# Two pieces of elementwise work in a decoder's mixers, moved from VectorE to GpSimd

## The chip, the core and the metric

The kernel runs on one core of a Trainium2 chip. The metric is the device time of one execution in microseconds (us). The engines named below are TensorE (PE: matmuls), VectorE (DVE), ScalarE (ACT), GpSimd (POOL) and SyncE (SP), which here only issues DMAs. Each engine runs its own list of instructions strictly in order; between engines there are semaphore waits.

## What is computed

One step of a two-layer decoder trunk for 256 prompt tokens and 64 sample tokens (8 sequences of 8). A layer is a SwiGLU feed-forward block, a block of four parallel mixers, and a second feed-forward block. The mixers read one input projection and feed one output projection:

```
proj = modulate(x, sh2, sc2) @ w_in[l]
u, v, xb, gate_b, gate_c, hc, glu_a, glu_g = split(proj)
ya = gelu(u) * (tril(w_s) @ layer_norm(gelu(v), ln_g, ln_b) + b_s)   # A
yb = (window_mean(xb, 2|4|8|16) - xb) @ pool_w * pool_scale          # B
yc = gate_b * conv3(gate_c * hc)                                     # C
yd = silu(layer_norm(conv31(glu_a * sigmoid(glu_g)) + b))            # D
x  = layer_norm(alpha*x + (1+g2) * rms_norm([ya|yb|yc|yd]) @ w_out[l])
```

The change touches two pieces: the running sums behind B's window means (each of four channel groups has its own window, 2, 4, 8 or 16 tokens), and the scale and offset `ln_g`, `ln_b` of A's values `v`.

## The kernel before

Activations lie with channels on the 128 partitions and the 320 tokens along the free axis. All weights are streamed from HBM once. Each weight unit (128 x 1024, fp32) is cut by ACT (L232, `whi`) and DVE (L240, `wlo` = `raw` - `whi`) into a high and a low part, and each product of TensorE is three matmuls. The weight units of the input projection are cut several units ahead of the matmuls that use them, and the order of all instructions is the order in which the Python code issues them; no scheduler moves them.

In a mixer block the projection's first five column groups are done together (`zcm`): D's two halves and the first half of B's input. ScalarE and VectorE form D's gated input `eD`, `cD` (L906 to L910), and ScalarE lays out a halo copy of it and makes tap 0 of the 31-tap convolution: `dtap0` (L914, L915), first for channel half 0, then for half 1, into the two accumulators `aD`. The other 30 taps of each half are 60 DVE instructions (L923), alternating between the halves, each reading `cD` and `aD` and adding into `aD`. ScalarE also copies B's input to `eB`, `eBs` (L940, L941).

The rest of the input projection is ten weight units: `hc0`, `xb1`, `up0`, `val` (two), `up1`, `gc0`, `gb0`, `gc1`, `hc1`, `gb1`. The list `MIX_SEQ` writes their order out by hand, with the other steps between them. At each new weight unit a hook adds to a `credit` the time that TensorE will need for the unit, less the cost of a split, and issues taps until the credit is used up; each step of `MIX_SEQ` then takes its price in `DVE_COST` off the credit. So the prices decide between which other DVE instructions the taps stand. The step `mean` issues all taps that are left, and then TensorE's matmuls `cmn` (L1116), which need both finished accumulators; TensorE issues nothing else until they are through. Behind `mean` come D's normalisation, C's taps, the group norms and the output projection `wo`.

The steps that the change touches:

- `pool0` and `pool1` (L946 to L969): for one channel half, the running sums over 2, 4 (or 2, 4, 8, 16) tokens by doubling, for prompt (L958) and samples (L959), and from them B's means less the input (L962 to L969). All on DVE. `pool0` stands first in `MIX_SEQ`, `pool1` far behind `mean`.
- `vgain` (`v_gain`, L1019): three tiles of 128 x 256 times `sgln[0]`, then plus `sgln[1]`: six DVE instructions, behind `mean`.
- `vstat`, `vnorm`: the values' statistics on DVE, a `pow` on POOL (L1012), then one DVE instruction (L1015) and three ScalarE instructions (L1017).

POOL does before the change only `pow` of 128 x 3 elements (L1012, L1132, L596, L367), four `affine_select` in the whole program (L438, L440), and memsets.

Of the kernel before, what the change touches and what calls it, by code (L numbers as in the profile page):

```python
# [67 lines left out]


MIX_SEQ = """  # L70
    pool0 hc0 xb1 up0 val vstat up1 gc0 gb0 vnorm cconv0 gc1 hc1 gb1 mean cconv1 sub sq4 ada6 ctaps0 ctaps1 cgate0
    cgate1 stat4 pow4 vgain ada2 sq2 bc4 norm swish stat2 sq3 sgu pow2 pool1 ada2 stat3 bc2 pow3 poolmm mul2 hi2
    sq1 sgate bc3 lo2 sq0 ada2 stat1 mul3 hi3 pow1 ko0 stat0 lo3 pow0 bc1 mul1 ko1 hi1 lo1 step step bc0 mul0 hi0
    ada18 ko2 lo0 ko3 ko4 ko5
""".split()
# [216 lines left out]
def sam(ap):  # L292
    return ap.rearrange("p (b t) -> p b t", t=NT_S)


class Kern:
# [568 lines left out]
    def mix_body(self, l, gb, G, late):  # L865
        nc, st, io, tp, mp = self.nc, self.st, self.io, self.t, self.mp
# [77 lines left out]

        yA, yB, yC, pl, gu, mix, vs = [], [], [], [], [], {}, {}

        def pool(j):
            e, es = eB[j], eBs[j]
            o = Y(f"pl{l}{j}")
            pl.append(o)  # L950
            sp = [mp.tile([P, 271], F32, tag="sp", bufs=2, name=f"s{i}p{l}{j}") for i in range(2)]
            ss = [mp.tile([P, NB, 23], F32, tag="ss", bufs=2, name=f"s{i}s{l}{j}") for i in range(2)]
            cp, cs_, sh = e, es, 1
            for g in range(2 * j + 2):
                np_, nss = sp[g % 2], ss[g % 2]
                lo = sh * 2 - 1
                p0 = 0 if g < 2 * j + 1 else 64
                V.tensor_tensor(np_[p0:P, lo:271], cp[p0:P, lo:271], cp[p0:P, lo - sh:271 - sh], op=ALU.add)  # L958
                V.tensor_tensor(nss[p0:P, :, lo:23], cs_[p0:P, :, lo:23], cs_[p0:P, :, lo - sh:23 - sh], op=ALU.add)  # L959
                if g // 2 == j:  # L960
                    q = slice(64 * (g % 2), 64 * (g % 2) + 64)
                    V.tensor_tensor(o[q, 0:16], np_[q, 15:31], self.inv[q, j, 0:16], op=ALU.mult)  # L962
                    V.scalar_tensor_tensor(o[q, 16:NP_], np_[q, 31:271], self.inv[q, j, 16:17], e[q, 31:271],
                                           op0=ALU.mult, op1=ALU.subtract)
                    V.scalar_tensor_tensor(sam(o[q, NP_:N]), nss[q, :, 15:23], self.inv[q, j, 16:17],
                                           es[q, :, 15:23], op0=ALU.mult, op1=ALU.subtract)
                cp, cs_ = np_, nss
                sh *= 2
# [12 lines left out]
        vb = []
# [37 lines left out]
        def v_gain():  # L1019
            for i, op in ((0, ALU.mult), (1, ALU.add)):  # L1020
                for b in range(3):
                    V.tensor_tensor(vb[b], vb[b], self.sgln[:, i, :], op=op)
            outs.append((io["o_vp"][l], vb[1]))
            outs.append((io["o_vs"][l], vb[2][64:128, :]))

# [144 lines left out]
        def taps_(n):  # L1170
            for _ in range(min(n, len(taps))):
# [4 lines left out]
               "gc": win(cgin), "hc": win(chin), "gb": win(cbin), "vstat": lambda _: v_stat(),  # L1176
               "vnorm": lambda _: v_norm(), "cconv": cconv, "t": taps_, "mean": mean, "sub": sub, "sq": sq, "stat": stat, "pow": pw_, "bc": bc, "mul": mul, "hi": hi, "lo": lo,
               "norm": norm, "swish": swish, "ctaps": ctaps, "cgate": cgate, "vgain": lambda _: v_gain(),
               "pool": pool, "poolmm": lambda _: pool_mm(), "sgu": lambda _: spatial(),
               "sgate": lambda _: spatial_gate(), "ko": ko, "ada": ada, "step": lambda _: self.ada_step()}  # L1180
        for nme, arg in MIX_OPS:
            ops[nme](arg)
            self.credit -= DVE_COST.get(nme, 0.0)
        st.ada(999)
# [245 lines left out]
```

## Time and profile before

| What | Value |
|---|---|
| device time, 3 runs | 1285.9 us median (1285.89 to 1292.28) |
| the profiled execution | 1289.18 us |
| its span, first to last instruction | 1287.4 us |
| mean granted TensorE clock | 0.99 |
| PE busy / DVE busy | 98% / 57% of the span |
| ACT busy / POOL busy | 43% / 2% of the span |
| layer 0: D's gated input done, `mean` on TensorE | 302.93 us, 350.96 us |
| layer 1: the same | 926.11 us, 975.46 us |

The span is 1.8 us shorter than the device time of the same execution, and that execution is 3.3 us above the median. Times within the trace count from the span's start. A row of the timeline gives the start, the duration, the engine, the line, the operation and the tiles; "x9" is nine equal instructions in a row, with the duration from the first's start to the last's end; the square bracket tells how long the engine was idle before, and whose instruction ended that.

### The profile page before, as it was taken

What the parts mean: (1) busy time and instruction counts of PE and PEld (TensorE: products, weight loads), DVE (VectorE), ACT (ScalarE), POOL (GpSimd) and SP (SyncE); (2) the same over time, 40 slices, a digit from 0 to 9 for tenths busy, and PEclk for the clock granted to TensorE, in tenths of its full rate; (3) what the DMA queues carried; (4) which work ended last, traced back from release to release, by engine and by line L of the source; (5) the groups of instructions that cost most, each with busy time, mean ns of one, the idle gap of its engine ahead of it and who ended that gap; (6) DMA issues with size and microseconds to landing.
All of it is one profiled execution on the core that took longest, in us unless ns stands there. A gap on an engine that the chain in (4) does not pass through costs nothing.

```text
span 1287.4 us, 22297 instructions
## 1 busy us (share of the span) xinstructions
PE 1263.3 (98%) x9414; PEld 1213.7 (94%) x9414; DVE 730.0 (57%) x1321; ACT 555.8 (43%) x872; POOL 22.4 (2%) x39
## 2 busy tenths in 40 slices
PE   9999999999999999999999999999997999999996
PEld 8999999999888999999999999999995989999996
DVE  5644444468977644453575454445798775454444
ACT  3643333347444643343445343333653455343332
POOL 0000000000010000000000000000000000000000
PEclk9999999999999999999999999999998989999999
DMA  9865556568849854534465555454775694434301
GB/s 376 315 233 211 196 198 255 198 213 240 303 182 94 327 180 148 211 135 162 164 216 209 173 187 201 176 201 171 222 256 197 104 236 164 155 140 164 131 1 41
DMA packets 63748, 247.46 MB, mean 192 GB/s; under 512 B 31072, under 2 KB 33632, under 8 KB 34464
## 3 DMA queue, kind: packets, MB, share of 16 engines
q1 hardware_dynamic: 58912, 245.11, 56.9%
q8 instruction: 74, 1.21, 0.4%
q10 hardware_dynamic: 4736, 0.93, 0.4%
q14 instruction: 26, 0.21, 0.0%
HBM read 243.45 MB, written 2.57 MB: 191 GB/s over the span
## 4 chain that ended last, share of the span: by engine, by line
PE 90%; DVE 6%; ACT 2%; DMA 1%; issue 1%; POOL 0%; ACTq 0%; another core or an unknown queue 0%; SPq 0%; DVEq 0%
PE of L672 4%; PE adp L466 4%; PE oh L673 4%; PE of L673 4%; PE oh L674 4%; PE of L674 4%; PE oh L672 4%; PE uf L672 4%; PE uh L674 4%; PE uh L672 4%; PE uf L673 4%; PE uf L674 4%; PE uh L673 4%; PE gf L672 4%; PE gh L672 3%; PE gh L674 3%
## 5 line engine op out<-in xcount | busy, mean ns | idle before, releaser
L240 DVE TENSOR_TENSOR wlo<-raw,whi 128x1024 fp32r<-128x1024 f32 x312 | 373.1, 1223 | 137.3 <-ACT whi L232 136.4
L232 ACT CAST whi<-raw 128x1024 fp32r<-128x1024 f32 x312 | 315.3, 1045 | 24.4 <-issue 8.4
L672 PE MATMUL of<-hhf,whi 128*128 128x320 f32 x352 | 109.4, 311 | 0.0
L674 PE MATMUL of<-hhf,wlo 128*128 128x320 f32 x352 | 108.9, 310 | 0.0
L673 PE MATMUL of<-hlf,whi 128*128 128x320 f32 x352 | 108.9, 309 | 0.0
L672 PE MATMUL oh<-hhh,whi 128*128 128x320 f32 x352 | 108.5, 308 | 0.0
L674 PE MATMUL oh<-hhh,wlo 128*128 128x320 f32 x352 | 108.5, 308 | 0.0
L673 PE MATMUL oh<-hlh,whi 128*128 128x320 f32 x352 | 108.5, 308 | 0.0
L672 PE MATMUL uf<-xhif,whi 128*128 128x320 f32 x320 | 99.3, 310 | 0.0
L672 PE MATMUL uh<-xhih,whi 128*128 128x320 f32 x320 | 98.9, 309 | 0.0
L674 PE MATMUL uf<-xhif,wlo 128*128 128x320 f32 x320 | 98.8, 309 | 0.0
L673 PE MATMUL uf<-xlof,whi 128*128 128x320 f32 x320 | 98.8, 309 | 0.0
L673 PE MATMUL uh<-xloh,whi 128*128 128x320 f32 x320 | 98.8, 309 | 0.0
L674 PE MATMUL uh<-xhih,wlo 128*128 128x320 f32 x320 | 98.8, 309 | 0.0
L672 PE MATMUL gf<-xhif,whi 128*128 128x320 f32 x304 | 94.5, 311 | 0.0
L672 PE MATMUL gh<-xhih,whi 128*128 128x320 f32 x304 | 94.1, 309 | 0.0
L674 PE MATMUL gf<-xhif,wlo 128*128 128x320 f32 x304 | 93.9, 309 | 0.0
L673 PE MATMUL gf<-xlof,whi 128*128 128x320 f32 x304 | 93.9, 309 | 0.0
L674 PE MATMUL gh<-xhih,wlo 128*128 128x320 f32 x304 | 93.9, 309 | 0.0
L673 PE MATMUL gh<-xloh,whi 128*128 128x320 f32 x304 | 93.8, 309 | 0.0
L775 ACT CAST hhh<-sgh 128x320 fp32r<-128x320 f32 x44 | 20.2, 459 | 134.3 <-DVE sgh L772 133.8
L775 ACT CAST hhf<-sgf 128x320 fp32r<-128x320 f32 x44 | 20.2, 459 | 134.3 <-DVE sgf L772 134.3
(334 smaller groups left out, 2806.5 us busy)
## 6 DMA issues: line engine op xcount, KB each, us to landing
raw<-in_w_main SPq DMA_DIRECT2D x156, 1024.0 KB, 5.0
raw<-in_w_ada SPq DMA_DIRECT2D x72, 1024.0 KB, 6.8
out_yT<-x SPq DMA_DIRECT2D x8, 160.0 KB, 1.8
xt<-in_x SPq DMA_DIRECT2D x2, 512.0 KB, 4.2
wsT<-in_wsT SPq DMA_DIRECT2D x2, 256.0 KB
sgln<-in_sgln SPq DMA_DIRECT2D x2, 256.0 KB, 5.1
cD<-in_pre_d SPq DMA_DIRECT2D x4, 120.0 KB, 8.4
out_o_ds<-cD ACTq DMA_DIRECT2D x4, 120.0 KB, 9.7
```

What stands on the lines that cost most here:

```text
L232: kk.nc.scalar.copy(hi, raw)
L240: self.kk.nc.vector.tensor_tensor(lo, raw, hi, op=ALU.subtract)
L466: nc.tensor.matmul(ps[32 * g:32 * g + 32, 0:w], self.cs[:, k, :], wt[:, h, g * w:(g + 1) * w], start=(k == 0), stop=(k == NK - 1))
L672: mm(ps, hi, xh, start=first, stop=False)
L673: mm(ps, hi, xl, start=False, stop=False)
L674: mm(ps, lo, xh, start=False, stop=last)
L775: nc.scalar.copy(hi, sg)
```

## The change

`pool` is cut in two. A new step `psum` (`pool_sums`) makes the running sums on GpSimd, and `pool` keeps the division by the window and the subtraction on VectorE. `MIX_SEQ` issues `psum0` first, `pool0` after `hc0`, and `psum1` after `xb1`; `pool1` keeps its place. The six instructions of `v_gain` go to GpSimd, and the step `vgain` goes from behind `mean` to right behind `vnorm`. The price of `pool` falls from 3.5 to 1.9; that of `vgain` stays 2.0, and `psum` has none.

```diff
 MIX_SEQ = """
-    pool0 hc0 xb1 up0 val vstat up1 gc0 gb0 vnorm cconv0 gc1 hc1 gb1 mean cconv1 sub sq4 ada6 ctaps0 ctaps1 cgate0
+    psum0 hc0 pool0 xb1 psum1 up0 val vstat up1 gc0 gb0 vnorm vgain cconv0 gc1 hc1 gb1 mean cconv1 sub sq4 ada6 ctaps0
...
-DVE_COST = {"pool": 3.5, "vstat": 1.3, "vnorm": 0.1, "cconv": 0.5, "ctaps": 1.2, "cgate": 0.4, "vgain": 2.0, "sgate": 1.0,
+DVE_COST = {"pool": 1.9, "vstat": 1.3, "vnorm": 0.1, "cconv": 0.5, "ctaps": 1.2, "cgate": 0.4, "vgain": 2.0, "sgate": 1.0,
...
+        def pool_sums(j):
+            add = nc.gpsimd.tensor_tensor
+            sp = [mp.tile([P, 271], F32, tag="sp", bufs=2, name=f"s{i}p{l}{j}") for i in range(2)]
+            ss = [mp.tile([P, NB, 23], F32, tag="ss", bufs=2, name=f"s{i}s{l}{j}") for i in range(2)]
+            cp, cs_, sh = eB[j], eBs[j], 1
+            for g in range(2 * j + 2):
+                np_, nss = sp[g % 2], ss[g % 2]
+                lo = sh * 2 - 1
+                p0 = 0 if g < 2 * j + 1 else 64
+                add(np_[p0:P, lo:271], cp[p0:P, lo:271], cp[p0:P, lo - sh:271 - sh], op=ALU.add)
+                add(nss[p0:P, :, lo:23], cs_[p0:P, :, lo:23], cs_[p0:P, :, lo - sh:23 - sh], op=ALU.add)
+                cp, cs_ = np_, nss
+                sh *= 2
+            sums[j] = sp, ss
...
         def pool(j):
...
-                V.tensor_tensor(np_[p0:P, lo:271], cp[p0:P, lo:271], cp[p0:P, lo - sh:271 - sh], op=ALU.add)
-                V.tensor_tensor(nss[p0:P, :, lo:23], cs_[p0:P, :, lo:23], cs_[p0:P, :, lo - sh:23 - sh], op=ALU.add)
...
+            sp, ss = sums.pop(j)
+            for h in range(2):
+                q = slice(64 * h, 64 * h + 64)
+                V.tensor_tensor(o[q, 0:16], sp[h][q, 15:31], self.inv[q, j, 0:16], op=ALU.mult)
...
         def v_gain():
             for i, op in ((0, ALU.mult), (1, ALU.add)):
                 for b in range(3):
-                    V.tensor_tensor(vb[b], vb[b], self.sgln[:, i, :], op=op)
+                    nc.gpsimd.tensor_tensor(vb[b], vb[b], self.sgln[:, i, :], op=op)
```

The instructions of TensorE and ScalarE stand in the same order before and after. On VectorE and GpSimd the order moves, in both layers alike, at three places. (A number behind a name is that of the tile.)

The first is VectorE in layer 0, from D's gated input on. Before:

```order
L910 TENSOR_TENSOR cD_2958<-zcm_2999,sgm_3211 128x8x8
L958 TENSOR_TENSOR s0p_3228<-eb_2961 128x270
L959 TENSOR_TENSOR s0s_3230<-esb_2962 128x8x22
L962 TENSOR_TENSOR pl_3227<-s0p_3228,inv 64x16
L963 SCALAR_TENSOR_TENSOR pl_3227<-s0p_3228,inv,eb_2961 64x240
L965 SCALAR_TENSOR_TENSOR pl_3227<-s0s_3230,inv,esb_2962 64x64
L958 TENSOR_TENSOR s1p_3229<-s0p_3228 64x268
L959 TENSOR_TENSOR s1s_3231<-s0s_3230 64x8x20
L962 TENSOR_TENSOR pl_3227<-s1p_3229,inv 64x16
L963 SCALAR_TENSOR_TENSOR pl_3227<-s1p_3229,inv,eb_2961 64x240
L965 SCALAR_TENSOR_TENSOR pl_3227<-s1s_3231,inv,esb_2962 64x64
L969 TENSOR_TENSOR pl_3227<-pl_3227,eb_2961 128x16
```

Behind these rows one tap and two splits follow. After, the first five taps stand behind `cD`, then come these rows:

```order
L923 SCALAR_TENSOR_TENSOR aD_3208<-cD_2958,par,aD_3208 128x320
L923 SCALAR_TENSOR_TENSOR aD_3207<-cD_2954,par,aD_3207 128x320
L240 TENSOR_TENSOR wlo_3237<-raw_2897,whi_3236 128x1024
L240 TENSOR_TENSOR wlo_3240<-raw_2897,whi_3239 128x1024
L972 TENSOR_TENSOR pl_3279<-s0p_3227,inv 64x16
L973 SCALAR_TENSOR_TENSOR pl_3279<-s0p_3227,inv,eb_2961 64x240
L975 SCALAR_TENSOR_TENSOR pl_3279<-s0s_3229,inv,esb_2962 64x64
L972 TENSOR_TENSOR pl_3279<-s1p_3228,inv 64x16
L973 SCALAR_TENSOR_TENSOR pl_3279<-s1p_3228,inv,eb_2961 64x240
L975 SCALAR_TENSOR_TENSOR pl_3279<-s1s_3230,inv,esb_2962 64x64
L977 TENSOR_TENSOR pl_3279<-pl_3279,eb_2961 128x16
```

Seven taps, of both halves, and two splits now stand where `pool0` stood, and what is left of `pool0` stands behind them.

The second is GpSimd in layer 0, behind the memsets of the mixer's tiles. Before:

```order
L888 MEMSET eb_2969 128x15
L888 MEMSET ec_2973 128x2
L1012 TENSOR_TENSOR rva_3218<-rva_3218,mhalf 128x3
L1132 TENSOR_TENSOR rv_3865<-rv_3865,mhalf 128x3
L1132 TENSOR_TENSOR rv_3920<-rv_3920,mhalf 128x3
```

After, from `psum1` on (the four instructions of `psum0` stand in front of these rows, the other three of `vgain` and the five `pow` of L1132 behind them):

```order
L959 TENSOR_TENSOR s0p_3346<-eb_2969 128x270
L960 TENSOR_TENSOR s0s_3348<-esb_2970 128x8x22
L959 TENSOR_TENSOR s1p_3347<-s0p_3346 128x268
L960 TENSOR_TENSOR s1s_3349<-s0s_3348 128x8x20
L959 TENSOR_TENSOR s0p_3346<-s1p_3347 128x264
L960 TENSOR_TENSOR s0s_3348<-s1s_3349 128x8x16
L959 TENSOR_TENSOR s1p_3347<-s0p_3346 64x256
L960 TENSOR_TENSOR s1s_3349<-s0s_3348 64x8x8
L1020 TENSOR_TENSOR rva_3218<-rva_3218,mhalf 128x3
L1030 TENSOR_TENSOR v_3523<-v_3523,sgln_2113 128x256
L1030 TENSOR_TENSOR v_3525<-v_3525,sgln_2113 128x256
L1030 TENSOR_TENSOR v_3527<-v_3527,sgln_2113 128x256
```

Eight additions stand in front of the values' `pow`, and `vgain` behind it. The sums of `psum1` take the buffers that `psum0` used, so the first of them waits until VectorE's `pool0` has read these.

The third is VectorE in layer 1, around the values' normalisation. Before:

```order
L240 TENSOR_TENSOR wlo_9939<-raw_9642,whi_9938 128x1024
L1015 SCALAR_TENSOR_TENSOR rva_9559<-mv_9558,rva_9559 128x3
L1073 TENSOR_TENSOR ec_9306<-hc_9584,gcs_9932 128x256
L1074 TENSOR_TENSOR esc_9307<-hc_9584,gcs_9932 128x8x8
L923 SCALAR_TENSOR_TENSOR aD_9549<-cD_9299,par,aD_9549 128x320
L923 SCALAR_TENSOR_TENSOR aD_9548<-cD_9295,par,aD_9548 128x320
```

A third tap and the next split follow. After:

```order
L240 TENSOR_TENSOR wlo_9954<-raw_9648,whi_9953 128x1024
L1023 SCALAR_TENSOR_TENSOR rva_9559<-mv_9558,rva_9559 128x3
L1081 TENSOR_TENSOR ec_9306<-hc_9576,gcs_9947 128x256
L1082 TENSOR_TENSOR esc_9307<-hc_9576,gcs_9947 128x8x8
L240 TENSOR_TENSOR wlo_10004<-raw_9648,whi_10003 128x1024
```

The three taps between C's product (`ec`, `esc`) and the next split are gone. The same stretch of layer 0 has eight taps there before and three after. At the end, before `mean`, layer 0 has 5 taps behind the last split but one and the last split behind these; after, two of the taps stand behind the last split. Layer 1 has 9 taps behind its last split before, and 10 after.

## Rows read from the trace of the kernel before

**Rows 1.** The page, busy time and share of the span by engine.

```profile
PE 1263.3 (98%) x9414; PEld 1213.7 (94%) x9414; DVE 730.0 (57%) x1321; ACT 555.8 (43%) x872; POOL 22.4 (2%) x39
```

**Rows 2.** Waits of PE: waiting line and releaser, us in total, times, longest.

```profile
PE cmn L1116 <- DVE aD L923: 5.7, 1, 5.7
...
PE rr L541 <- ACT sqrm L834: 2.2, 2, 1.1
...
PE rr L611 <- POOL rv L1132: 0.6, 2, 0.3
```

**Rows 3.** Timeline of PE, `mean` and the next statistics, layers 0 and 1.

```profile
350.96 1.24 PE L1116 MATMUL cmn<-aD,o 128*128 128x320 f32 x4
...
354.86 1.55 PE L541 MATMUL rr<-o,sqrm 128*128 128x64 f32 x12
...
975.46 2.50 PE L1116 MATMUL cmn<-aD,o 128*128 128x320 f32 x4 [5.74 <-DVE aD L923]
...
982.36 1.55 PE L541 MATMUL rr<-o,sqrm 128*128 128x64 f32 x12
```

**Rows 4.** Windows, layer 1: stretch, length, busy by engine, granted clock, DMA, GB/s.

```profile
970.00:972.00 2.00, 0.00 (x0) 0.00 (x0) 2.00 (x4) 0.18 (x1) 0.00 (x0) 1.00 0.00 0
...
976.00:978.00 2.00, 2.00 (x8) 0.78 (x10) 0.33 (x2) 0.75 (x2) 0.00 (x0) 0.50 0.03 8
```

**Rows 5.** Timeline of DVE, first evacuation of the output projection, layers 0 and 1.

```profile
388.76 0.23 DVE L824 TENSOR_TENSOR evsm<-wo,ada 128x64 f32<-128x64 f32 x1 [0.36 <-PE wo L674]
...
1014.74 0.23 DVE L824 TENSOR_TENSOR evsm<-wo,ada 128x64 f32<-128x64 f32 x1 [0.37 <-PE wo L674]
```

**Rows 6.** Timeline of DVE, layer 1, from D's gated input on.

```profile
926.11 0.43 DVE L958 TENSOR_TENSOR s0p<-eb 128x270 f32<-128x270 f32 x1
...
926.71 0.16 DVE L962 TENSOR_TENSOR pl<-s0p,inv 64x16 f32<-64x16 f32 x1
...
927.46 0.43 DVE L958 TENSOR_TENSOR s1p<-s0p 64x268 f32<-64x268 f32 x1
...
928.05 0.17 DVE L962 TENSOR_TENSOR pl<-s1p,inv 64x16 f32<-64x16 f32 x1
...
930.84 2.36 DVE L240 TENSOR_TENSOR wlo<-raw,whi 128x1024 fp32r<-128x1024 f32 x2 [1.36 <-ACT whi L232]
```

**Rows 7.** Timeline of ACT, layer 1, tap 0 of D's two halves.

```profile
927.21 0.66 ACT L915 ACTIVATE aD<-cD,par 128x320 f32<-128x320 f32 x1
...
929.12 0.66 ACT L915 ACTIVATE aD<-cD,par 128x320 f32<-128x320 f32 x1
```

**Rows 8.** Timeline of DVE, layer 1, taps and splits.

```profile
933.12 4.25 DVE L923 SCALAR_TENSOR_TENSOR aD<-cD,par,aD 128x320 f32<-128x320 f32 x9
...
961.13 1.47 DVE L923 SCALAR_TENSOR_TENSOR aD<-cD,par,aD 128x320 f32<-128x320 f32 x3
964.04 1.23 DVE L240 TENSOR_TENSOR wlo<-raw,whi 128x1024 fp32r<-128x1024 f32 x1 [1.44 <-ACT whi L232]
```

**Rows 9.** Timeline of DVE and ACT, layer 0, the last taps and a cast.

```profile
339.66 3.78 DVE L923 SCALAR_TENSOR_TENSOR aD<-cD,par,aD 128x320 f32<-128x320 f32 x8
...
347.62 2.40 DVE L923 SCALAR_TENSOR_TENSOR aD<-cD,par,aD 128x320 f32<-128x320 f32 x5
...
341.75 1.05 ACT L232 CAST whi<-raw 128x1024 fp32r<-128x1024 f32 x1
```

**Rows 10.** Timeline of POOL and DVE around two `affine_select`; last, a free `G`.

```profile
824.22 0.63 POOL L438 TENSOR_SCALAR_AFFINE_SELECT wsT<-wsT 128x512 f32<-128x512 f32 x1 [169.04 <-DMA wsT<-in_wsT]
824.82 1.61 POOL L440 TENSOR_SCALAR_AFFINE_SELECT wsS<-wsS 128x256 f32<-128x256 f32 x1
...
822.00 3.94 DVE L240 TENSOR_TENSOR wlo<-raw,whi 128x1024 fp32r<-128x1024 f32 x3 [0.46 <-ACT whi L232]
825.86 0.63 DVE L531 TENSOR_SCALAR G<-ada 128x72 f32<-128x72 f32 x1
...
202.42 0.19 DVE L531 TENSOR_SCALAR G<-ada 128x72 f32<-128x72 f32 x1
```

**Rows 11.** Timeline of DVE, layer 1, `vgain`.

```profile
984.03 2.09 DVE L1022 TENSOR_TENSOR v<-v,sgln 128x256 f32<-128x256 f32 x6
```

More of the change, by code (lines that the diff above doesn't have):

```diff
@@ L70 @@
 MIX_SEQ = """
-    pool0 hc0 xb1 up0 val vstat up1 gc0 gb0 vnorm cconv0 gc1 hc1 gb1 mean cconv1 sub sq4 ada6 ctaps0 ctaps1 cgate0
-    cgate1 stat4 pow4 vgain ada2 sq2 bc4 norm swish stat2 sq3 sgu pow2 pool1 ada2 stat3 bc2 pow3 poolmm mul2 hi2
+    psum0 hc0 pool0 xb1 psum1 up0 val vstat up1 gc0 gb0 vnorm vgain cconv0 gc1 hc1 gb1 mean cconv1 sub sq4 ada6 ctaps0
+    ctaps1 cgate0 cgate1 stat4 pow4 ada2 sq2 bc4 norm swish stat2 sq3 sgu pow2 pool1 ada2 stat3 bc2 pow3 poolmm mul2 hi2
     sq1 sgate bc3 lo2 sq0 ada2 stat1 mul3 hi3 pow1 ko0 stat0 lo3 pow0 bc1 mul1 ko1 hi1 lo1 step step bc0 mul0 hi0
@@ L945, in mix_body @@
         yA, yB, yC, pl, gu, mix, vs = [], [], [], [], [], {}, {}
+        sums = {}
+        def pool_sums(j):
[12 more added lines that the diff above has]
+            sums[j] = sp, ss
         def pool(j):
@@ L950, in pool @@
             pl.append(o)
[L951 to L957, printed above, removed]
-                V.tensor_tensor(np_[p0:P, lo:271], cp[p0:P, lo:271], cp[p0:P, lo - sh:271 - sh], op=ALU.add)
-                V.tensor_tensor(nss[p0:P, :, lo:23], cs_[p0:P, :, lo:23], cs_[p0:P, :, lo - sh:23 - sh], op=ALU.add)
[L960 to L968, printed above, removed]
+            sp, ss = sums.pop(j)
+            for h in range(2):
+                q = slice(64 * h, 64 * h + 64)
+                V.tensor_tensor(o[q, 0:16], sp[h][q, 15:31], self.inv[q, j, 0:16], op=ALU.mult)
+                V.scalar_tensor_tensor(o[q, 16:NP_], sp[h][q, 31:271], self.inv[q, j, 16:17], e[q, 31:271],
+                                       op0=ALU.mult, op1=ALU.subtract)
+                V.scalar_tensor_tensor(sam(o[q, NP_:N]), ss[h][q, :, 15:23], self.inv[q, j, 16:17],
+                                       es[q, :, 15:23], op0=ALU.mult, op1=ALU.subtract)
             V.tensor_tensor(o[:, 0:16], o[:, 0:16], e[:, 15:31], op=ALU.subtract)
@@ L1178, in mix_body @@
                "norm": norm, "swish": swish, "ctaps": ctaps, "cgate": cgate, "vgain": lambda _: v_gain(),
-               "pool": pool, "poolmm": lambda _: pool_mm(), "sgu": lambda _: spatial(),
+               "pool": pool, "psum": pool_sums, "poolmm": lambda _: pool_mm(), "sgu": lambda _: spatial(),
                "sgate": lambda _: spatial_gate(), "ko": ko, "ada": ada, "step": lambda _: self.ada_step()}
```

## The prediction, made before the changed kernel was run

> **What bounds the kernel now.** I read the busy shares first. PE is busy for 98% of the span [rows 1], so work taken off VectorE can only show where PE waits for it. The waits of PE name that place: one wait of 5.7 us for D's taps at `mean`, and nothing else of that size [rows 2]. The timeline of PE shows that it is layer 1's: `cmn` starts at 975.46 after 5.74 us of idling, while layer 0's starts at 350.96 with no wait [rows 3]. The wait costs more than its length. PE's granted clock was 1.00 while it idled and 0.50 (the lower of its two levels, 1.2 GHz) when it worked again [rows 4], and from `cmn` to the next statistics layer 1 took 982.36 - 975.46 = 6.90 us where layer 0 took 354.86 - 350.96 = 3.90 us [rows 3]. So the change is worth what it does to the moment when the last taps end, in each layer. In layer 1 every microsecond on VectorE ahead of that counts fully. Layer 0 has little room: its last five taps run from 347.62 to 350.02 [rows 9]; PE needs the first accumulator, done one tap earlier, at 349.55, and arrives at 350.96: 1.41 us to spare.
>
> **What is removed.** Ahead of `mean` only `pool0`'s sums leave VectorE: two pairs, 926.11 to 926.71 and 927.46 to 928.05 [rows 6], 0.60 + 0.59 = 1.19 us per layer. `vgain` (2.09 us for six instructions, [rows 11]) and `pool1`'s eight sums stood behind `mean`. What PE waits for there is ScalarE's squares (2.2 us in both layers together) and a `pow` of GpSimd (0.6 us) [rows 2]; none is a VectorE queue, so I take their removal as worth 0, at most 2.8 us.
>
> **What the new order costs.** A tap of a row takes 4.25/9 = 0.47 us [rows 8].
>
> At the start, before, VectorE filled the time with `pool0` and waited only 1.36 us for a cast [rows 6]. Now taps come first, and tap 1 of a half needs ScalarE's tap 0 of it, done at 927.21 + 0.66 = 927.87 and 929.12 + 0.66 = 929.78 [rows 7]. VectorE is free at 926.11: it waits 1.76 us, does one tap until 928.34, and waits 1.44 us again. That is 3.20 us against 1.36: +1.84 us. The two splits come behind the taps, by then their casts are done. Layer 0 has the same pattern at 303 us; I take the same figure.
>
> In the middle, the value normalisation on ScalarE waits for VectorE's `vnorm`, and behind it in ScalarE's queue stand C's first tap and the next cast, for which VectorE's next split waits. In layer 1 three taps (1.47 us) filled that time, and 1.44 us of waiting was left [rows 8]. Now no tap stands there: 1.41 us more waiting. In layer 0 eight taps (3.78 us from 339.66) covered it wholly. With three, VectorE is through at 339.66 + 3 x 0.47 = 341.07, and the cast ends at 341.75 + 1.05 = 342.80 [rows 9]; all shift alike, so 1.73 us of waiting is new.
>
> At the end of layer 0 a split moves ahead of the last two taps: 1.14 us (two take 2.36, [rows 6], one 1.23, [rows 8]).
>
> Sums without any effect of GpSimd on VectorE: layer 1, -1.19 + 1.84 + 1.41 = +2.06 us. Layer 0, -1.19 + 1.84 + 1.73 + 1.14 = +3.52 us, less 1.41 to spare = 2.11 us of new waiting.
>
> **What GpSimd's work does to VectorE.** The trace has one place where GpSimd reads tiles of this width while VectorE works: two `affine_select` at 824.22 and 824.82 [rows 10]. They hold each other up. Three splits took 3.94 us; by two in 2.36 [rows 6] they would take 3.50. The scalar multiply behind them took 0.63 us, and 0.19 where GpSimd was idle [rows 10]. So each `affine_select` held one VectorE instruction for 0.44 us, and the second, which takes about 0.63 itself, took 1.61 because it waited for a split. Taps and splits all read two SBUF tiles, as these splits do.
>
> No row has an addition of two such tiles on GpSimd. The low end of what one holds is 0, since it cannot make VectorE faster. The high end is 2 x 0.44 = 0.88 us, if two streams take twice as long as one. I take 0.44: the nearest row, of 512 and 256 columns. `psum0` runs while VectorE waits for `aD` and costs nothing. `psum1` starts when `pool0` has read the buffers; from there VectorE has taps and splits without a gap, so all eight collide. `vgain` starts behind `vnorm`; most of its six fall into the wait for the cast, which absorbs them, and I count one. 9 x 0.44 = 3.96 us per layer.
>
> The Trainium skill (SBUF — State Buffer, Who interferes with whom) has the rule that speaks against this change: a VectorE instruction with two SBUF inputs and a GpSimd instruction that reads SBUF take turns, and the loser is blocked for the whole instruction. The trace agrees that they take turns, and shows 0.44 of 0.63 us. With whole instructions the sum would be 9 x 0.19 x 2 = 3.4 us larger.
>
> **What is queued behind.** `pool0` on VectorE waits for `psum0`, long done by then. The values' `pow` stands behind `psum1` on GpSimd's queue, which is through some microseconds earlier. Behind the late `vnorm` ScalarE's queue holds, in layer 0, a copy that TensorE's conditioning matmuls need; PE will wait there, but what is left of its projection still ends before the taps, so this is a part of the wait, not one more. The splits run several units ahead of their matmuls; 5 us later hurts none. SyncE's loads are released by the splits, later by the same few microseconds.
>
> **The sum.** Layer 0: 2.11 + 3.96 = 6.07 us of waiting, of about the length of layer 1's before, so I expect its slow stretch too. Layer 0's own later stretches count against that: from `cmn` to the first evacuation it took 388.76 - 350.96 = 37.80 us and layer 1, slow at `mean`, 1014.74 - 975.46 = 39.28 [rows 3, 5], so the slow clock costs 1.48 us net. Layer 1: 2.06 + 3.96 = 6.02 us; its slow stretch is there already. Together 13.6 us: the profiled execution would go from 1289.2 to 1302.8, and the median, 3.3 us lower, from 1285.9 to 1299.5.
>
> **Rivals.**
> (1) GpSimd does not hold up VectorE, say because its reads fit between VectorE's. Against: the rows of 824 us. Then 2.11 + 2.06 = 4.2 us, 1290.1, and with a slow stretch in layer 0 up to 1.5 us more.
> (2) An addition holds twice as long, 0.88 us: 7.92 instead of 3.96 us per layer, +7.9: 1307.4. For: two inputs instead of one. Against: half the columns of the first `affine_select`.
> (3) Not slower: the relief is what counts. If the two starts and the cast were not late, because ScalarE gets ahead when VectorE does, only the removed sums are left in layer 1: -1.2, 1284.7. It decides from the point where new waits on ScalarE stay under 1.19 us per layer; I find 3.25 us in layer 1. If the work behind `mean` counted too, another 2.8 us: 1281.9; and layer 1's slow stretch of 3.0 us with it would be needed to pass 0.5% (1279.5).
>
> **How the numbers follow.** A measurement of this kernel can tell about 0.5%, 6.4 us, from no change: 1279.5 to 1292.3. The forecast, 1299.5 with its own range of 1293 to 1306, has 0.62. Rival 2 has 0.13, rival 1 0.17, rival 3 0.08 (0.04 of it below 1279.5, with what I can't name). Slower by over 0.5%: 0.62 + 0.13 and the slow end of rival 1, 0.01, is 0.76; the same 0.20; faster 0.04. The range leaves out rival 3 and the far end of rival 2: 1289.5 to 1308.
>
> **What would show it.** In the changed kernel's timeline of VectorE: two waits for `aD` behind `cD`, a wait of about 2.9 us (layer 1) before the split behind `esc`, splits and taps of 0.44 us more during `psum1`, and GpSimd's additions of 0.6 us with waits on top. In PE's waits: `cmn` in both layers, about 6 and 12 us, or in layer 0 a part of it at the conditioning matmuls. Granted clock 0.5 around layer 0's `mean`. I am wrong if `cmn` of layer 1 starts less than 49.3 us after D's gated input, if splits keep 1.14 us beside GpSimd's additions, or if PE waits at a place not named here.

## The result, and the profile after

The kernel before took 1288.66 us (median of 8 runs, 1285.89 to 1294.05), the changed one 1299.07 us (8 runs, 1295.88 to 1300.64): 10.4 us more, a ratio of 1.0069 with a 95% interval of 1.005 to 1.0088. The change makes the kernel slower. The span of the profiled execution went from 1287.4 to 1298.5 us.

The page's busy line of the changed kernel answers [rows 1]. VectorE has 36 instructions fewer and GpSimd 36 more. VectorE's busy time fell by 1.5 us only, GpSimd's rose by 26:

```profile
PE 1265.8 (97%) x9414; PEld 1216.9 (94%) x9414; DVE 728.5 (56%) x1285; ACT 556.0 (43%) x872; POOL 48.3 (4%) x75
```

The waits of PE in the changed kernel (waiting line and releaser, us in total, times, longest) answer [rows 2]. The one wait for the taps has doubled, from 5.7 to 11.4 us, and a wait for `adev`, ScalarE's copy for the conditioning matmuls, is new:

```profile
PE cmn L1124 <- DVE aD L923: 11.4, 1, 11.4
PE adp L489 <- ACT adev L485: 3.5, 2, 2.8
...
PE rr L541 <- ACT sqrm L834: 2.2, 2, 1.1
...
PE rr L611 <- POOL rv L1140: 0.4, 2, 0.2
```

The timeline of PE in the changed kernel, to be read against [rows 3]: in layer 0 the wait stands at `adp`, and `cmn` starts without one; in layer 1 it stands at `cmn`.

```profile
346.75 1.07 PE L489 MATMUL adp<-sel,adev 128*128 128x36 f32 x4 [2.77 <-ACT adev L485]
...
357.17 1.34 PE L1124 MATMUL cmn<-aD,o 128*128 128x320 f32 x4
...
986.86 2.50 PE L1124 MATMUL cmn<-aD,o 128*128 128x320 f32 x4 [11.38 <-DVE aD L923]
```

Windows of the changed kernel in layer 0 (stretch, length, busy PE, PEld, DVE, ACT, POOL, granted clock, DMA, GB/s): behind the wait for `adev` PE works on at half clock, the lower level, until about 353, some 4 us before `mean`.

```profile
346.00:350.00 4.00, 3.25 (x13) 3.26 (x14) 3.23 (x4) 3.85 (x7) 4.00 (x5) 0.51 0.92 387
350.00:354.00 4.00, 4.00 (x20) 4.00 (x19) 4.00 (x7) 0.00 (x0) 0.80 (x1) 0.64 0.79 266
354.00:358.00 4.00, 4.00 (x26) 3.69 (x25) 4.00 (x9) 0.48 (x2) 0.00 (x0) 1.00 0.12 16
```

Where the time goes is read from the timeline of VectorE in the changed kernel, layer 1, against [rows 6], [rows 8] and these further rows of the kernel before, a split, four taps and five taps:

```profile
937.29 1.21 DVE L240 TENSOR_TENSOR wlo<-raw,whi 128x1024 fp32r<-128x1024 f32 x1
938.42 1.93 DVE L923 SCALAR_TENSOR_TENSOR aD<-cD,par,aD 128x320 f32<-128x320 f32 x4
...
941.41 2.39 DVE L923 SCALAR_TENSOR_TENSOR aD<-cD,par,aD 128x320 f32<-128x320 f32 x5
```

In the changed kernel there are two waits for `aD` at the start; from 941.39 on instructions that are longer than before (five taps in 3.77 us, where five took 2.39); a wait of 2.83 us for the cast in the middle; then a split of 1.40 us and four taps in 2.87, where four took 1.93.

```profile
933.66 0.55 DVE L923 SCALAR_TENSOR_TENSOR aD<-cD,par,aD 128x320 f32<-128x320 f32 x1 [1.71 <-ACT aD L915]
935.57 2.87 DVE L923 SCALAR_TENSOR_TENSOR aD<-cD,par,aD 128x320 f32<-128x320 f32 x6 [1.36 <-ACT aD L915]
...
941.39 0.61 DVE L972 TENSOR_TENSOR pl<-s1p,inv 64x16 f32<-64x16 f32 x1
941.93 0.75 DVE L973 SCALAR_TENSOR_TENSOR pl<-s1p,inv,eb 64x240 f32<-64x240 f32 x1
...
943.41 3.77 DVE L923 SCALAR_TENSOR_TENSOR aD<-cD,par,aD 128x320 f32<-128x320 f32 x5
...
973.86 1.40 DVE L240 TENSOR_TENSOR wlo<-raw,whi 128x1024 fp32r<-128x1024 f32 x1 [2.83 <-ACT whi L232]
975.19 2.87 DVE L923 SCALAR_TENSOR_TENSOR aD<-cD,par,aD 128x320 f32<-128x320 f32 x4
```

And GpSimd's timeline beside it: the long VectorE rows are those that GpSimd's additions overlap. Its own additions take 0.64 us for 270 columns at first, 0.88 for 264 when VectorE has taps without a gap.

```profile
931.64 0.64 POOL L959 TENSOR_TENSOR s0p<-eb 128x270 f32<-128x270 f32 x1 [21.36 <-ACT esb L941]
...
941.33 0.64 POOL L959 TENSOR_TENSOR s0p<-eb 128x270 f32<-128x270 f32 x1 [7.49 <-DVE pl L973]
...
943.82 0.88 POOL L959 TENSOR_TENSOR s0p<-s1p 128x264 f32<-128x264 f32 x1
...
971.35 5.44 POOL L1030 TENSOR_TENSOR v<-v,sgln 128x256 f32<-128x256 f32 x6 [10.15 <-ACT v L1025]
```

The table cuts the span of every kernel of this study at the same events, from one profiled execution each: D's gated input done (start of the second `cD` plus 0.13 us), start of `cmn`, first evacuation of the output projection (`evsm`). Each column is a length in us. The rows below the second are the experiments of the next section.

| kernel | to gated, layer 0 | gated to `mean` | `mean` to evacuation | to gated, layer 1 | gated to `mean` | `mean` to evacuation | to the end |
|---|---|---|---|---|---|---|---|
| before | 302.93 | 48.03 | 37.80 | 537.35 | 49.35 | 39.28 | 272.66 |
| after | 303.27 | 53.90 | 37.81 | 536.89 | 54.99 | 39.88 | 271.76 |
| order alone | 303.40 | 50.17 | 36.27 | 536.91 | 51.34 | 39.95 | 271.76 |
| sums alone | 303.48 | 54.12 | 37.82 | 542.35 | 52.01 | 40.60 | 272.52 |
| gain alone | 303.68 | 50.86 | 37.70 | 535.88 | 51.90 | 40.53 | 271.45 |
| work gone | 303.70 | 48.03 | 37.70 | 535.88 | 49.35 | 39.90 | 271.74 |
| adds beside | 305.10 | 49.58 | 47.45 | 536.92 | 55.26 | 38.06 | 271.03 |
| kinds beside | 303.46 | 48.03 | 36.26 | 537.01 | 50.52 | 38.25 | 270.87 |
| statistics late | 304.78 | 48.01 | 44.09 | 540.24 | 46.10 | 38.78 | 271.10 |
| late and filled | 303.94 | 48.02 | 45.40 | 540.22 | 44.68 | 44.18 | 274.96 |
| sums, copy first | 303.22 | 51.39 | 36.27 | 536.09 | 51.60 | 40.78 | 270.95 |
| after, copy first | 303.94 | 55.06 | 37.68 | 535.87 | 54.94 | 39.16 | 272.65 |
| waits filled | 303.52 | 48.03 | 37.81 | 538.25 | 46.79 | 39.54 | 271.56 |

The second row less the first: 0.34 + 5.87 + 0.01 - 0.46 + 5.64 + 0.60 - 0.90 = 11.1 us. The loss is where the two layers go from the gated input to `mean`, 11.5 us together. The other columns differ from kernel to kernel where nothing was edited, mostly by a microsecond or two, the stretch to layer 1 by up to 6.5 (535.9 to 542.4 us), so the two columns up to `mean` are the ones to read; a total can move by that much by itself. Where the taps are done before TensorE comes to `mean` in layer 0 (before, work gone, kinds beside, waits filled), its column repeats to the hundredth (48.03).

### The profile page after: what moved, and what is told of

It is laid out like the page before. It is cut to its first block, busy times and chain, and to the rows that moved or that the text cites. A ratio compares the mean times of both kernels' runs of the same rounds, so it can differ in the third digit from the quotient of the medians.

```text
span 1298.5 us, 22314 instructions
## 1 busy us (share of the span) xinstructions
PE 1265.8 (97%) x9414; PEld 1216.9 (94%) x9414; DVE 728.5 (56%) x1285; ACT 556.0 (43%) x872; POOL 48.3 (4%) x75
## 3 DMA queue, kind: packets, MB, share of 16 engines
q8 instruction: 74, 1.21, 0.4%
## 4 chain that ended last, share of the span: by engine, by line
PE 68%; issue 19%; DVE 8%; ACT 2%; DMA 1%; POOL 0%; POOLq 0%; ACTq 0%; SPq 0%
PE of L672 4%; PE of L673 4%; PE of L674 4%; PE uf L672 4%; PE uf L674 4%; PE uf L673 4%; DVE aD L923 4%; PE gf L672 3%; PE gf L674 3%; PE gf L673 3%; PE adp L466 3%; DVE wlo L240 2%; PE oh L674 2%; PE oh L673 2%; PE oh L672 2%
```

## The experiments

**The order alone.** GpSimd's new work left out, the order of VectorE as after the change:

```diff
 def pool_sums(j):
-    ...
-            add(np_[p0:P, lo:271], cp[p0:P, lo:271], cp[p0:P, lo - sh:271 - sh], op=ALU.add)
-    ...
-    sums[j] = sp, ss
+    sums[j] = (eB[j], eB[j]), (eBs[j], eBs[j])
 def v_gain():
-    for i, op in ((0, ALU.mult), (1, ALU.add)):
-        ...
```

> The changed kernel with GpSimd's new work left out: the running sums are not made (the means are taken from the input itself) and the values get no scale and offset. VectorE's list of instructions is that of the changed kernel, row by row. Theory (new order plus what GpSimd holds up): only the order is left. D's gated input to `mean` in layer 1: 51.4 us (before 49.35, after 54.99), PE's wait there 7.8 us; no tap, split or `pool0` instruction longer than in the kernel before; in layer 0 2 us of waiting. In all 4 to 6 us slower than before, 1.003 to 1.0045. Rival 1 (GpSimd holds nothing up, the order alone costs what was lost): as slow as the changed kernel, +10 us, 1.008.

Measured: 1.0019 (1.0003 to 1.0036). The trace has the predicted places: gated input to `mean` 51.34 us in layer 1 and 50.17 in layer 0. First the waits of PE, then VectorE's five taps behind `pool0` and the split in the middle, layer 1:

```profile
PE cmn L1109 <- DVE aD L923: 9.2, 2, 7.7
```
```profile
937.12 2.40 DVE L923 SCALAR_TENSOR_TENSOR aD<-cD,par,aD 128x320 f32<-128x320 f32 x5
...
966.21 1.23 DVE L240 TENSOR_TENSOR wlo<-raw,whi 128x1024 fp32r<-128x1024 f32 x1 [2.83 <-ACT whi L232]
```

The taps are back at 2.40 us, the wait for the cast is still 2.83. So the waits belong to the order and the long taps to GpSimd, and rival 1 (the order alone costs it all) is out. The order costs 2.0 us in layer 1 and 2.1 in layer 0; the rest of the changed kernel's loss, 54.99 - 51.34 = 3.65 and 53.90 - 50.17 = 3.73 us, comes with GpSimd's work. The total, 2.4 us in the trace, was below the 4 to 6 us expected: layer 0 had no slow stretch behind `mean` in this trace (36.27 against 37.80), and the end was 0.9 us shorter.

**The work gone, the old order.** What would moving the work bring if GpSimd cost nothing?

```diff
 def pool(j):
-    V.tensor_tensor(np_[p0:P, lo:271], cp[p0:P, lo:271], cp[p0:P, lo - sh:271 - sh], op=ALU.add)
-    V.tensor_tensor(nss[p0:P, :, lo:23], cs_[p0:P, :, lo:23], cs_[p0:P, :, lo - sh:23 - sh], op=ALU.add)
 def v_gain():
-    V.tensor_tensor(vb[b], vb[b], self.sgln[:, i, :], op=op)
```

> The kernel before in its old order, with all the moved work simply left out: no running sums, no scale and offset of the values, on any engine. It is the most that moving them could bring. Theory: only `pool0`'s sums stand ahead of a wait of PE, and only in layer 1: 1.2 us less there (gated input to `mean` 48.2 us), nothing behind `mean`: 1 to 2 us faster than before, 0.9985 to 0.999. Rival 3 (relief of VectorE behind `mean` counts too): 4 us or more, 0.997 or less.

Measured: 0.9994 (0.9972 to 1.0016), no difference. Neither theory was right in the trace: gated input to `mean` is 48.03 and 49.35 us, to the hundredth as before. PE's waits and VectorE's first splits in layer 1:

```profile
PE cmn L1109 <- DVE aD L923: 5.7, 1, 5.7
```
```profile
930.04 2.36 DVE L240 TENSOR_TENSOR wlo<-raw,whi 128x1024 fp32r<-128x1024 f32 x2 [2.38 <-ACT whi L232]
```

In [rows 6] the wait in front of these splits was 1.36 us; it has become 2.38. `pool0` stood in a gap in which VectorE had to wait for ScalarE anyway, and its sums were worth nothing. Behind `mean` 4.3 us of VectorE's work per layer went away too, and the stretch to the evacuation is not shorter than in [rows 3, 5] by more than 0.1 us. In the old order there was nothing to gain.

**The two halves of the change.** The sums alone, with `vgain` back on VectorE behind `mean`:

```diff
-    psum0 hc0 pool0 xb1 psum1 up0 val vstat up1 gc0 gb0 vnorm vgain cconv0 ...
+    psum0 hc0 pool0 xb1 psum1 up0 val vstat up1 gc0 gb0 vnorm cconv0 ...
-    ... stat4 pow4 ada2 ...
+    ... stat4 pow4 vgain ada2 ...
-                    nc.gpsimd.tensor_tensor(vb[b], vb[b], self.sgln[:, i, :], op=op)
+                    V.tensor_tensor(vb[b], vb[b], self.sgln[:, i, :], op=op)
```

> The changed kernel, but `vgain` back on VectorE and behind `mean`. Theory: of the order's costs the start stays (1.7 us), the wait for the cast in the middle goes (four taps there in layer 1, seven in layer 0), and of the hold only that of the sums, 2.5 us in layer 1. Layer 1: gated input to `mean` 51.9 us (+2.6); layer 0: 1.8 us of waiting at `mean`. In all 4.4 to 5.9 us slower than before, 1.0035 to 1.0045. Rival 1: without a hold +0.1 in layer 1 and nothing in layer 0, 1.000.

Measured: 1.0048 (1.0029 to 1.0066), just above what was expected. Layer 1 as expected, 52.01 us. Layer 0 was not in this trace: 6.1 us instead of 1.8, and not for the taps. Its timeline, PE, then VectorE's last taps and the subtraction that waits for `cmn`:

```profile
346.97 1.07 PE L489 MATMUL adp<-sel,adev 128*128 128x36 f32 x4 [2.79 <-ACT adev L485]
```
```profile
352.68 1.01 DVE L923 SCALAR_TENSOR_TENSOR aD<-cD,par,aD 128x320 f32<-128x320 f32 x2
...
358.88 0.89 DVE L1128 TENSOR_TENSOR aD<-aD,cmn 128x320 f32<-128x320 f32 x2 [3.58 <-PE cmn L1124]
```

The taps were done at 353.7, and VectorE waited 3.58 us for TensorE, which had waited for ScalarE's copy and then worked at the lower clock. The profiled execution was the slowest of this kernel's runs (1304.6, median 1296.6), so this holds for it and is not shown for a typical one.

The gain alone is the kernel before with `vgain` on GpSimd, right behind `vnorm`:

```diff
-    ... gb0 vnorm cconv0 ... stat4 pow4 vgain ada2 ...
+    ... gb0 vnorm vgain cconv0 ... stat4 pow4 ada2 ...
-                    V.tensor_tensor(vb[b], vb[b], self.sgln[:, i, :], op=op)
+                    nc.gpsimd.tensor_tensor(vb[b], vb[b], self.sgln[:, i, :], op=op)
```

> The kernel before, but `vgain` on GpSimd and right behind `vnorm`, at its price of 2.0; the sums stay on VectorE. Theory: no tap fills the wait for the cast in layer 1 (2.85 us instead of 1.44) and the hold is 1.1 us: gated input to `mean` 51.9 us (+2.5). Layer 0: 1.7 us at the cast, 1.1 of a split moved ahead of the last taps, 1.2 of hold, less 1.4 to spare: 2.6 us, seen at the conditioning matmuls or at `mean`. In all 5.1 to 6.6 us slower than before, 1.004 to 1.005; with the run of the sums alone it adds up to the changed kernel's +10. Rival 1: without a hold 1.4 + 1.4 = 2.8 us, 1.002.

Measured: 1.0027 (1.0009 to 1.0046), below the 1.004 to 1.005 expected; layer 1 51.90 us as expected, layer 0 2.8 us longer, where TensorE waits for the taps:

```profile
354.54 2.50 PE L1116 MATMUL cmn<-aD,o 128*128 128x320 f32 x4 [2.68 <-DVE aD L923]
```

In layer 1 the two halves come to 2.66 + 2.55 = 5.21 of the 5.64 us of the whole. In layer 0 of these two traces they do not add up: 6.09 and 2.83 against 5.87, because in the one the copy came late, in the other the taps, and TensorE waits for the later of two. In the medians they about do: 0.0048 and 0.0027 make 0.0075, the whole has 0.0069.

**GpSimd beside VectorE, by itself.** The kernel before, with idle instructions on GpSimd next to the taps:

```diff
+        def dummies():
+            d = mp.tile([P, 256], F32, name=f"dum{l}")
+            e, G = eB[1], nc.gpsimd
+            G.tensor_tensor(d[:, 0:1], e[:, 270:271], e[:, 269:270], op=ALU.add)
+            for _ in range((8, 16)[l]):
+                G.tensor_tensor(d, e[:, 15:271], e[:, 14:270], op=ALU.add)
-    pool0 hc0 xb1 up0 ...
+    pool0 hc0 xb1 dum up0 ...
```

> The kernel before, with idle additions put on GpSimd (two inputs, 128x256, results unused; one of 128x1 ahead of them), released by the copy of `xb1` to `eb`: 8 in layer 0, 16 in layer 1. VectorE's list is that of the kernel before. Theory: each holds one VectorE instruction for about 0.32 us (2.53 us for the eight sums of `psum1` in the changed kernel; predicted had been 0.44), in proportion to their number: in layer 1 `mean` 5.1 us later (gated input to `mean` 54.5 us), in layer 0 VectorE 2.5 us later, of which 1.1 us or a little more shows. Rival 1 (no hold): 49.35 us in layer 1, time as before. Rival 2 (0.88 us each): 14 us in layer 1.

Timeline of layer 1, GpSimd and VectorE (before, nine taps took 4.25, a split 1.21, four taps 1.93, five 2.39):

```profile
948.59 15.31 POOL L952 TENSOR_TENSOR dum<-eb 128x256 f32<-128x256 f32 x16
```
```profile
946.07 5.32 DVE L923 SCALAR_TENSOR_TENSOR aD<-cD,par,aD 128x320 f32<-128x320 f32 x9
951.31 1.63 DVE L240 TENSOR_TENSOR wlo<-raw,whi 128x1024 fp32r<-128x1024 f32 x1
952.86 3.36 DVE L923 SCALAR_TENSOR_TENSOR aD<-cD,par,aD 128x320 f32<-128x320 f32 x4
956.14 1.63 DVE L240 TENSOR_TENSOR wlo<-raw,whi 128x1024 fp32r<-128x1024 f32 x1
957.70 4.18 DVE L923 SCALAR_TENSOR_TENSOR aD<-cD,par,aD 128x320 f32<-128x320 f32 x5
961.80 1.63 DVE L240 TENSOR_TENSOR wlo<-raw,whi 128x1024 fp32r<-128x1024 f32 x1
963.36 2.75 DVE L923 SCALAR_TENSOR_TENSOR aD<-cD,par,aD 128x320 f32<-128x320 f32 x5
```

VectorE lost 1.07 + 0.42 + 1.43 = 2.92 us to the eight additions of layer 0 (the first three rows there have the same lengths) and 1.07 + 0.42 + 1.43 + 0.42 + 1.79 + 0.42 + 0.36 = 5.91 us to the sixteen of layer 1: 0.37 us each in both, a little more than the 0.32 expected. `mean` came the same 5.91 us later in layer 1. The hold is there, in proportion to the number; rivals 1 and 2 are out.

The total, 1.0099 (1.0072 to 1.0126), is more than these two delays. In layer 0 `mean` came only 1.6 us later, but the stretch behind it took 47.45 instead of 37.80 us. Timelines of GpSimd and PE there, and two windows:

```profile
360.80 2.64 POOL L1139 TENSOR_TENSOR rv<-rv,mhalf 128x3 f32<-128x3 f32 x1 [25.68 <-DVE rv L1138]
```
```profile
363.49 1.54 PE L611 MATMUL rr<-ident,rv 128*128 128x128 f32 x6 [2.26 <-POOL rv L1139]
```
```profile
364.00:368.00 4.00, 4.00 (x20) 3.88 (x19) 1.25 (x4) 2.17 (x5) 0.13 (x1) 0.50 1.01 428
...
376.00:380.00 4.00, 4.00 (x15) 3.41 (x15) 1.75 (x6) 0.52 (x1) 0.85 (x1) 0.50 0.00 0
```

A `pow` of three columns took 2.64 us instead of 0.96, while VectorE made its six instructions of `vgain` in one go (2.08 us from 360.64). PE waited 2.26 us for it and then worked at half clock for some 17 us, until about 380. Why the `pow` lost here and not in the kernel before, where the same six stand beside it, is open.

The other kinds, in the same place:

```diff
+            for _ in range(8):
+                if l == 0:
+                    G.memset(d, 0.0)
+                else:
+                    G.tensor_scalar(d, e[:, 15:271], 1.0, None, op0=ALU.add)
```

> The kernel before, with eight idle GpSimd instructions at the same place, of another kind in each layer: in layer 0 memsets of 128x256 (nothing read), in layer 1 additions of a constant (one input of 128x256). Theory (what GpSimd reads takes turns with VectorE's two inputs): layer 0 as before, 48.03 us from gated input to `mean` and no longer tap; layer 1 as with two inputs, 0.3 to 0.44 us each as the two `affine_select` of the trace before, so `mean` 2.4 to 3.5 us later. Rival (only a second input holds VectorE up): both layers as before.

Measured: 0.9991 (0.9969 to 1.0013). Timelines of GpSimd and VectorE, layer 0 (memsets), then layer 1 (one input):

```profile
312.81 2.90 POOL L953 MEMSET dum<- 128x256 f32 x8
...
934.31 9.43 POOL L955 TENSOR_SCALAR dum<-eb 128x256 f32<-128x256 f32 x8
```
```profile
310.31 4.25 DVE L923 SCALAR_TENSOR_TENSOR aD<-cD,par,aD 128x320 f32<-128x320 f32 x9
314.47 1.22 DVE L240 TENSOR_TENSOR wlo<-raw,whi 128x1024 fp32r<-128x1024 f32 x1
...
937.35 2.21 DVE L923 SCALAR_TENSOR_TENSOR aD<-cD,par,aD 128x320 f32<-128x320 f32 x4
```

The memsets run from 312.81 to 315.71, beside the last of these nine taps and the split, and both keep the lengths of before (4.25 and 1.2 us). Beside one-input instructions the taps lose a little: four take 2.21 us instead of 1.93, and `mean` comes 1.17 us later for eight, 0.15 us each, less than half of what a two-input addition takes and below what I expected. So it is GpSimd's reading that holds VectorE up. The Trainium skill (SBUF — State Buffer, Who interferes with whom) says that a VectorE instruction with two SBUF inputs contends with a GpSimd instruction that reads SBUF, not with one that only writes it; the trace agrees (0 against 0.15 and 0.37 us). The Trainium skill (SBUF — State Buffer, Terms) also says that the port pair which the two engines share is held for the full instruction and that the loser fully blocks. That is not what these rows show: an addition held VectorE for 0.37 us, and one of 270 columns took 0.64 us in the changed kernel, at 931.64, as VectorE went into its wait for `aD`.

**TensorE's copy in layer 0.** Was it the copy that cost the sums alone 6.1 us? `vnorm` goes behind `gc1`, so that ScalarE makes the copy first:

```diff
-    ... gc0 gb0 vnorm cconv0 gc1 hc1 gb1 mean ...
+    ... gc0 gb0 cconv0 gc1 vnorm hc1 gb1 mean ...
```

> The run of the sums alone, with `vnorm` issued behind `gc1` instead of ahead of `cconv0`, so that ScalarE makes the copy for the conditioning matmuls ahead of the values' normalisation. Theory (in the run of the sums alone layer 0 lost its 6.1 us to that copy and to the half clock behind it, not to the taps, which were done 4 us before TensorE came): the wait of 2.8 us for `adev` goes, TensorE reaches `mean` when the taps are done, 50 us from gated input to `mean` in layer 0 instead of 54.1; layer 1 51 to 52. 4 us less than the run of the sums alone: 1.001 to 1.0025. Rival (VectorE's delay sets layer 0's loss whatever ScalarE does): 53.5 us or more in layer 0, 1.0045 or more.

Measured: 1.0042 (1.0022 to 1.0062). In the trace layer 0 fell to 51.39 us, 2.7 less; a wait of 1.56 us for the copy was left, because C's first tap, which waits for VectorE's `ec`, still stands ahead of it. But the medians of the two kernels are the same within 0.3 us (1296.41 and 1296.63). The 4 us did not come in the time. The profiled execution was the fastest of this kernel's runs (1292.0) and the other one the slowest of its kernel's (1304.6), so what the typical run does there stays open.

The same edit in the changed kernel (`vnorm` and `vgain` behind `gc1`):

> The changed kernel with the same edit: `vnorm` and `vgain` behind `gc1`, so that the copy for the conditioning matmuls comes first on ScalarE. Theory (in the changed kernel taps and copy come out at the same moment in layer 0, the copy's wait is a part of the taps' wait, as predicted): TensorE waits at `mean` instead, 52.5 to 54 us from gated input to `mean` in layer 0 (53.9 in the changed kernel), 54 to 55 in layer 1: within 2 us of the changed kernel, 1.0055 to 1.008. Rival (the copy alone costs layer 0 its 5.9 us): 50 to 51 us there, 1.003 to 1.005.

Measured: 1.009 (1.0062 to 1.0118). PE's timeline in layer 0:

```profile
359.00 2.50 PE L1124 MATMUL cmn<-aD,o 128*128 128x320 f32 x4 [5.06 <-DVE aD L923]
```

With the copy early, TensorE waits 5.06 us for the taps, and `mean` comes 55.06 us after the gated input: a microsecond above the range given, and far from the rival's 50 to 51. The edit also moves VectorE's wait for a cast one split on and lengthens it, from 0.77 to 2.52 us, so its taps are not quite those of the changed kernel. But that kernel's own rows say the same. Its last two taps in layer 0, one of each half:

```profile
356.58 1.00 DVE L923 SCALAR_TENSOR_TENSOR aD<-cD,par,aD 128x320 f32<-128x320 f32 x2
```

The first accumulator is done at about 357.1, and `cmn` starts at 357.17. In the changed kernel the taps alone would have cost layer 0 its loss; the copy is not on top of it.

**Versions that might be faster.** Nothing goes to GpSimd; the statistics and `vnorm`, which stand ahead of `mean`, go behind it:

```diff
-    ... val vstat up1 gc0 gb0 vnorm cconv0 gc1 hc1 gb1 mean cconv1 sub sq4 ada6 ctaps0 ctaps1 cgate0
+    ... val up1 gc0 gb0 cconv0 gc1 hc1 gb1 mean cconv1 sub sq4 ada6 vstat ctaps0 ctaps1 vnorm cgate0
```

> The kernel before with nothing moved to GpSimd; instead the values' statistics and `vnorm` stand behind `mean` (`vstat` behind `ada6`, `vnorm` behind `ctaps1`). Theory (only VectorE's time ahead of `mean` in layer 1 counts): 1.8 us of statistics and up to 1.4 us of the wait for the cast go: gated input to `mean` in layer 1 46 to 47.5 us instead of 49.35, PE's wait there 2.5 to 4 us instead of 5.7; layer 0 unchanged at 48.0. In all 2 to 4 us faster than before, 0.997 to 0.9985. Rival (the chain of statistics, `pow`, normalisation and gain comes due behind `mean`): a new wait of PE at the spatial matmuls of 2 us or more in each layer, no gain or a loss.

> As the run with the late statistics, and the price of `pool` 1.9 instead of 3.5, so that four taps and not one stand between `pool0` and the first two splits, where VectorE waited 1.36 us for the cast. Theory: 0.9 to 1.3 us more is gained ahead of `mean` in layer 1: 45 to 46.5 us from gated input to `mean`; in all 3 to 5 us faster than before, 0.996 to 0.998. Rival: ScalarE's tap 0 of the other half is not there for these taps, and the wait only changes its name: as the run without it.

Measured: 1.004 (1.0015 to 1.0065) and 1.0074 (1.0048 to 1.0099), both slower. Ahead of `mean` they did what was expected or a little more (46.10 and 44.68 us in layer 1), but the rival won behind it. PE's timeline in layer 0 of the first, and a window:

```profile
361.17 0.88 PE L611 MATMUL rr<-ident,rv 128*128 128x128 f32 x6 [1.93 <-POOL rv L1132]
```
```profile
368.00:372.00 4.00, 4.00 (x19) 3.42 (x19) 0.18 (x1) 0.00 (x0) 0.00 (x0) 0.50 0.00 2
```

VectorE's statistics delay D's `pow`; PE waits 1.93 us and then works at half clock until about 376: the stretch took 44.09 instead of 37.80 us. In the second kernel layer 1 has it too (44.18).

The last one changes two prices only:

```diff
-DVE_COST = {"pool": 3.5, "vstat": 1.3, "vnorm": 0.1, ...
+DVE_COST = {"pool": 1.9, "vstat": 1.3, "vnorm": -1.4, ...
```

> The kernel before with nothing moved to another engine and two prices changed: `pool` 1.9 instead of 3.5 and `vnorm` -1.4 instead of 0.1. In layer 1 four taps (one before) then stand between `pool0` and the first splits and seven (three before) in the middle, where VectorE waited 1.36 and 1.44 us for ScalarE's casts. Theory (what counts is how VectorE's waits ahead of `mean` in layer 1 are filled, not how much work it has): 1.0 + 1.4 us less ahead of `mean`: 46.9 us from gated input to `mean` in layer 1 instead of 49.35, PE's wait 3.3 instead of 5.7; layer 0 48.0 as before. 2 to 4 us faster than before, 0.997 to 0.9985. Rival: the taps taken forward make the splits behind them late for TensorE, a new wait for `wlo`: 1.000 or slower.

Measured: 0.9985 (0.9964 to 1.0006). VectorE's timeline in layer 1 and PE's wait:

```profile
931.32 1.48 DVE L923 SCALAR_TENSOR_TENSOR aD<-cD,par,aD 128x320 f32<-128x320 f32 x3 [0.32 <-ACT aD L915]
...
962.99 3.31 DVE L923 SCALAR_TENSOR_TENSOR aD<-cD,par,aD 128x320 f32<-128x320 f32 x7
```
```profile
PE cmn L1116 <- DVE aD L923: 3.2, 1, 3.2
```

Both waits for casts are filled, and `mean` comes 2.56 us earlier in layer 1, with VectorE doing exactly the work of before. It is faster than the changed kernel (their ranges do not meet); against the kernel before its 1.9 us by the ratio are within what can be told.

## Why the prediction was right, and where its sizes were off

The direction, the mechanism and the place were right, and 1299.07 us is next to the 1299.5 forecast. That closeness is partly luck. The forecast was 13.6 us above the kernel before; measured were 10.4, and the ratio's interval is 6.4 to 11.3 us. The median from which I started, 1285.9 of three runs, became 1288.66 with eight. By its steps:

- **What bounds it.** Right: all of the loss lies between the gated input and `mean`, and work behind `mean` was worth 0 (the work-gone run). One reading of the clock was too simple: it was 0.83 from 974 to 975 us in the kernel before, so it fell within the wait and not when PE worked again; nothing in the sum hangs on it.
- **What is removed, and the start.** -1.19 + 1.84 was right as a pair: the order alone cost 2.0 us in layer 1 where 2.06 were worked out. As a gain by itself the -1.19 was wrong. Left out in the old order, the sums bring 0.00, since `pool0` filled a wait for ScalarE. Rival 3 was priced at -1.2 us for the relief of layer 1; in the old order that relief was worth zero.
- **The middle and the end.** Right: the wait for the cast in layer 1 was 2.83 us (about 2.9 forecast), and the order alone cost layer 0 2.14 us (2.11 forecast).
- **GpSimd's hold.** Forecast 3.96 us per layer; it is 3.65 and 3.73 by the difference to the order alone. Its parts were off against each other. In layer 1: `pool0`'s own instructions were held too (2.79 us instead of 1.64 = 1.15), the taps behind them 1.38, together 2.53 us for the eight sums, where 8 x 0.44 = 3.52 had been taken; and `vgain` cost 1.11 us (0.17 of a split, 0.94 of four taps), not 0.44: its six instructions take 5.44 us and reach beyond the wait that was to absorb them. An addition of 128x256 holds 0.37 us, so 0.44 was a little high, and four of the eight sums are smaller.
- **TensorE's copy in layer 0.** "A part of the wait, not one more" held in the changed kernel, but by a hair: PE came to `mean` at 357.17, and the first accumulator was done at 356.58 + 0.5 = 357.1 by the row above. The wait was at `adp` (2.77 us), and the rest went into half clock behind it. In the trace of the sums alone it was false: PE came 3.9 us after the taps.
- **The clock: the term that was mis-sized.** I added 1.48 us for a slow stretch behind layer 0's `mean`. It came ahead of it, inside the wait: the conditioning matmuls, hc1 and gb1 took 357.17 - 346.75 = 10.42 us instead of 350.96 - 343.48 = 7.48, and those 2.94 us cost nothing more, since the taps ended no earlier. Behind `mean` layer 0 took 37.81 us, as before. With 1.47 there, 0.58 us less in the two layers' waits, and -0.42 us from the stretches I had left alone (0.34 - 0.46 + 0.60 - 0.90), the 13.6 become the 11.1 of the span.

## What to carry to other kernels

Before you move work off an engine, leave it out altogether and look at the wait that the engine had behind it: work that stands in a gap is free, and the 36 instructions moved here were worth nothing in the order that the kernel had. When the target engine reads the same memory, count what it takes from the engine you meant to relieve (0.37 us per two-input addition of 128x256 on GpSimd, beside VectorE's two-input instructions), and let a row of idle duplicates measure it. And where an order has waits for a third engine in it, fill them first: two changed prices gave 2.56 us at the place where moving the work lost 5.64, though the whole kernel's time does not yet tell that from no change.

## What had not been expected of the hardware

- A wait of TensorE of about 2 us can cost more than three times its length. Behind 1.93 us (the late statistics) and 2.26 us (the idle additions) the granted clock was 0.50 for some 14 and 17 us, and the stretch from `mean` to the evacuation grew by 6.3 and 9.7 us, the wait included; behind the 5.74 us at layer 1's `mean` the clock was 0.50 for some 7 us, and the kernel before lost 3.0. In the first two cases the statistics and spatial matmuls followed the wait. Why the clock stayed down so much longer there is open.
- GpSimd can lose as well: in one trace a `pow` of 128x3 took 2.64 us instead of 0.96 beside six VectorE instructions of two inputs.
- GpSimd's memsets of 128x256 (0.36 us each) took nothing from VectorE; its one-input instructions 0.15 us each, though they ran longer (1.18 us) than the two-input additions (0.91 to 0.96).
